# Hybrid attention block on one core: query and key projected with channels on partitions, rotated across partitions and carried to the scores through DRAM, the sliding heads placed amid the dilated pairs

## The chip, the core and the metric

The kernel runs on one core of one Trainium2 chip. The core has five engines with a program each: TensorE (PE, matmuls, with weight loads shown as PEld), VectorE (DVE), ScalarE (ACT), GpSimd (POOL) and SyncE (SP), which here issues every transfer between DRAM and on-chip memory. Sixteen DMA engines carry the transfers. Operands live in SBUF, matmul results in eight banks of PSUM. The metric is the device time of one execution in microseconds (us), the median of several runs.

## The reference

One layer of a decoder block: sequence 1024, width 1024, float32. Two sub-layers, each with an adaptive normalization ahead and a gated residual behind.

```python
h = rms_norm(x, g_attn_pre[l]) * (1 + sc_a) + sh_a
proj = h @ w_in[l]                       # 1024 x 2304
qa = partial_rope(proj[..., :o1] ...)    # mixer A: 8 query heads, 2 key heads, 2 value heads of 64
ka = partial_rope(...); va = ...
qb, kb = partial_rope(...), partial_rope(...); vb = ...   # mixer B: 8 heads of each
oa = banded_attention(qa, ka, va, 127, sink=sink_a[l])    # sliding window with sinks
ob = dilated_mixture_attention(qb, kb, vb)                # windows (128,1), (512,4), (2048,16)
mixed = concatenate([rms_norm(oa, g_mix_a[l]), rms_norm(ob, g_mix_b[l])])
y = mixed @ w_out[l]
x = x + gt_a * rms_norm(y, g_attn_post[l])
h = rms_norm(x, g_mlp_pre[l]) * (1 + sc_m) + sh_m
y = square(relu(h @ w_up[l])) @ w_down[l]
x = x + gt_m * rms_norm(y, g_mlp_post[l])
```

`partial_rope` turns the first 16 of the 64 channels of each head: channel f of the first eight is paired with channel f + 8, and both are mixed with the cosine and sine of the position. The dilated mixture is computed as one dense causal attention in which a mask adds the logarithm of the number of branches that see a key.

## The kernel before

Products are made in pairs of float32r halves: each operand is split into a high part and the rest, and three matmuls (high x high, high x low, low x high) stand for one. So a projection step over 128 of the 1024 channels (index k) is three matmuls.

The program isn't written in the order in which it runs. A planner (`Sched`, `run`) holds a queue of steps for each engine, with a duration, dependencies, buffers taken and given back (`Res`) and a priority, and writes the instructions out in the order of its own clock. PE has several streams (`dense`, `s`, `t`, `pv`, `post`, `misc` and others); `prefer` (L1932) chooses among them. SP's order is chosen in the same way, by the time at which a transfer can be issued. On the chip each engine then runs its list strictly in that order and waits where an operand isn't there. The planner counts a transfer as bytes over 345 GB/s plus fixed latencies.

The stages:

- To about 24 us: x is loaded, normalized and transposed to xnT; the modulation of the first sub-layer is computed on DVE (`mod_chunk`). The activations are kept in `hw` as [tile of 128 tokens][high, low].
- Input projection, 24 to 419 us. The output channels are cut into six units u of 384: units 0 to 3 hold two heads of mixer B each (two queries, two keys, two values), 4 and 5 one key head of mixer A with its four query heads. For each unit and each of eight tiles of 128 tokens, `proj_tile` (L805) makes [128 tokens x 384 channels] in one PSUM bank with 8 x 3 matmuls (`proj_mm`, L772): activations stationary, weights moving. `first_unit` (L783) does unit 0 over all eight banks as the activations become ready.
- `evac` (L673) empties each such bank: values are split into high and low parts (L687, L692); queries and keys are turned in place, channels along the free dimension (L703 to L707); they are split (L714 to L721); then PE transposes them to [channels x tokens], queries at L728 and keys at L740 (high and low parts, the key twice so that it fills 128 partitions), and ACT or DVE copies them to the rings `qring` and `kring`.
- Attention, mixed with the projection: 48 items. For mixer B an item is a pair of query blocks tp of one head h of unit u (`s_b`, L979), with pieces of up to 512 keys in two 256-wide halves (L1005); for mixer A it is one block of 128 queries for four heads (`s_a_`, L1038). Each goes through scores on PE, mask and maximum on DVE, exponential on ACT, normalization on POOL, then for each chunk of 256 keys (`t_pv`, L1097) four transposes (L1108 to L1115), a split (L1122, L1126) and the matmuls with the values (L1139 to L1150). Outputs go to DRAM (`o_dram`). The order of items (L955) is units 0 to 3, then the sliding heads, units 4 and 5.
- Output projection (`out_block`, L1294), eight blocks of tokens, each of 16 steps of three 512-wide matmuls (L1356 to L1358). Its weights are scaled and split into `hw` by `load_wo` (L1217), into the slot of each token tile once the last unit is done with that tile. A block starts when the items of its tokens are stored (`feed_out`, L1277).
- MLP, from 537.9 us: seven products for each of eight halves (`product`, L1746; L1780 to L1782), 512 wide. This change doesn't touch it.

POOL meanwhile computes the other modulation vectors from `w_ada` (`ada_piece`, L873).

## Time and profile before

| | us |
|---|---|
| runs | 1170.17, 1166.41, 1170.56 |
| median of 3 | 1170.17 |
| the profiled execution | 1170.0 |
| its span, first to last instruction | 1168.2 |
| PE busy in it | 1128.0 |
| DVE busy | 882.1 |
| ACT busy | 667.1 |
| POOL busy | 221.4 |
| bytes moved by DMA | 166.51 MB |

How to read the rows: a busy share says how long instructions were in flight, and matmuls overlap, so a PE that is busy isn't thereby at its peak; what a matmul costs in a stream is the distance from its start to the next start. "Idle before" in a group is the time for which the engine had nothing in flight just before these instructions, with what ended it. In the windows view each row is a stretch of the span with the busy time of each engine in it, the granted clock of PE (1.00 is full), the mean busy share of the 16 DMA engines, and the rate. In the DMA view a row gives the packets, their bytes, and for each kind of transfer the median time from its issue to its landing.

### The profile page before, as it was taken

How to read it: one execution, taken by the hardware profiler on the slowest of the kernel's cores; microseconds unless marked ns; L12 is line 12 of the kernel's file. 1: busy time of each engine (PE TensorE's matmuls, PEld its weight loads, DVE VectorE, ACT ScalarE, POOL GpSimd, SP SyncE). 2: the span in 40 equal slices, each digit the busy share in tenths (PEclk: the TensorE clock that was granted, in tenths of full speed). 3: DMA queues.
4: the chain of work that ended last, by engine and by line, in shares of the span. 5: the costliest groups of instructions: out<-in, count | busy, mean ns of one | idle time of the engine just before them, and what ended most of it. 6: DMA issues, size and time to landing. Idle time of an engine off the chain costs nothing.

```text
span 1168.2 us, 17209 instructions
## 1 busy us (share of the span) xinstructions
PE 1128.0 (97%) x5992; PEld 979.7 (84%) x5992; DVE 882.1 (76%) x1801; ACT 667.1 (57%) x1400; POOL 221.4 (19%) x270
## 2 busy tenths in 40 slices
PE   8989999999999979998999999999999999999996
PEld 6879999999999867887788888888888888888885
DVE  8987777777798996668969764499653796637998
ACT  7767666566667785666667434463234733256542
POOL 1044465555644431112000000000000000000002
PEclk9989999999999999999999999999999999999998
DMA  9613224222223324464584147922359311585103
GB/s 343 224 37 98 61 80 123 68 89 74 89 64 93 91 59 158 155 223 181 190 322 155 36 163 274 340 61 91 109 207 320 131 54 59 195 291 195 37 19 144
DMA packets 77542, 166.51 MB, mean 143 GB/s; under 512 B 6800, under 2 KB 27408, under 8 KB 77456
## 3 DMA queue, kind: packets, MB, share of 16 engines
q1 hardware_dynamic: 77456, 165.42, 41.4%
q8 instruction: 47, 0.77, 0.3%
q14 instruction: 39, 0.32, 0.1%
HBM read 137.08 MB, written 28.31 MB: 142 GB/s over the span
## 4 chain that ended last, share of the span: by engine, by line
PE 75%; DVE 13%; issue 4%; ACT 3%; POOL 2%; DMA 2%; SPq 0%; DVEq 0%; POOLq 0%; ACTq 0%
PE mlp_ps L1781 16%; PE mlp_ps L1782 16%; PE mlp_ps L1780 16%; PE pj L775 4%; PE pj L776 3%; PE pj L778 3%; PE s_ps L1005 3%; PE o_ps L1139 2%; PE pt_ps L1108 1%; PE pt_ps L1111 1%; DVE hw L1551 1%; PE pk L740 1%; DVE ph L1126 1%; PE y_ps L1356 1%; PE o_ps L1144 1%
## 5 line engine op out<-in xcount | busy, mean ns | idle before, releaser
L1780 PE MATMUL mlp_ps<-hw 128*128 128x512 f32 x896 | 350.3, 391 | 0.4 <-ACT hw L1542 0.4
L1781 PE MATMUL mlp_ps<-hw 128*128 128x512 f32 x896 | 349.1, 390 | 1.1 <-DVE hw L1548 1.1
L1782 PE MATMUL mlp_ps<-hw 128*128 128x512 f32 x896 | 348.9, 389 | 0.0
L1781 PEld LDWEIGHTS mlp_ps<-hw 128*128 128x128 f32 x896 | 168.5, 188 | 36.9 <-DVE hw L1548 1.4
L1780 PEld LDWEIGHTS mlp_ps<-hw 128*128 128x128 f32 x896 | 168.5, 188 | 36.1 <-ACT hw L1542 0.8
L1782 PEld LDWEIGHTS mlp_ps<-hw 128*128 128x128 f32 x896 | 168.4, 188 | 35.0
L1551 DVE TENSOR_TENSOR hw<-w,hw 128x1024 fp32r<-128x1024 f32 x96 | 114.6, 1220 | 94.7 <-ACT hw L1544 94.5
L1544 ACT CAST hw<-w 128x1024 fp32r<-128x1024 f32 x96 | 97.5, 1047 | 129.8 <-PE mlp_ps L1782 93.1
L1880 POOL TENSOR_TENSOR st<-st,nhalf 128x1 f32<-128x1 f32 x8 | 7.8, 979 | 602.8 <-DVE st L1878 602.8
L775 PE MATMUL pj<-w_hl,hw 128*128 128x384 f32 x320 | 118.2, 369 | 2.3 <-DVE sk L721 2.2
L776 PE MATMUL pj<-w_hl,hw 128*128 128x384 f32 x320 | 108.6, 339 | 1.2 <-DVE w_hl L497 1.1
L778 PE MATMUL pj<-w_hl,hw 128*128 128x384 f32 x320 | 108.5, 339 | 0.0
L1544 ACT CAST hw<-u 128x1024 fp32r<-128x1024 f32 x48 | 48.7, 1051 | 64.6 <-PE mlp_ps L1782 64.6
L1126 DVE TENSOR_TENSOR ph<-pt_ps,ph 128x512 fp32r<-128x512 f32 (+1 forms) x110 | 69.1, 643 | 17.6 <-ACT ph L1122 16.8
L1551 DVE TENSOR_TENSOR hw<-u,hw 128x1024 fp32r<-128x1024 f32 x48 | 57.0, 1218 | 18.2 <-ACT hw L1544 18.2
L1122 ACT CAST ph<-pt_ps 128x512 fp32r<-128x512 f32 (+1 forms) x110 | 59.3, 559 | 17.1 <-PE pt_ps L1111 13.3
L1035 POOL TENSOR_SCALAR p_sb<-p_sb,den 128x128 f32<-128x128 f32 (+3 forms) x64 | 51.3, 806 | 85.9 <-DVE den L1033 49.3
L1838 DVE TENSOR_TENSOR yacc<-yacc,mlp_ps 128x512 f32<-128x512 f32 x96 | 62.2, 681 | 3.3 <-PE mlp_ps L1782 3.3
L775 PEld LDWEIGHTS pj<-w_hl,hw 128*128 128x128 f32 x320 | 60.7, 190 | 3.6 <-DVE sk L721 3.1
L776 PEld LDWEIGHTS pj<-w_hl,hw 128*128 128x128 f32 x320 | 61.0, 191 | 2.7 <-DVE w_hl L497 2.1
L778 PEld LDWEIGHTS pj<-w_hl,hw 128*128 128x128 f32 x320 | 60.5, 189 | 0.0
L1030 ACT ACTIVATE p_sb<-p_sb,mn 128x128 f32<-128x128 f32 (+3 forms) x64 | 49.9, 780 | 17.4 <-DVE mn L1023 15.6
(206 smaller groups left out, 2167.3 us busy)
## 6 DMA issues: line engine op xcount, KB each, us to landing
hw<-s_dram SPq DMA_DIRECT2D x84, 512.0 KB, 4.4
wa_st<-in_w_ada SPq DMA_DIRECT2D x32, 512.0 KB, 4.3
w<-in_w_up SPq DMA_DIRECT2D x32, 512.0 KB, 5.2
w<-in_w_down SPq DMA_DIRECT2D x32, 512.0 KB, 7.7
s_dram<-hw SPq DMA_DIRECT2D x28, 512.0 KB, 3.8
w_st<-in_w_in SPq DMA_DIRECT2D x48, 192.0 KB, 3.8
x_sb<-in_x SPq DMA_DIRECT2D x16, 512.0 KB, 5.6
wa<-in_ada_t SPq DMA_DIRECT2D x16, 512.0 KB, 8.0
```

What stands on the lines that cost most here:

```text
L775: T.matmul(ps, hw[:, tb, 0, t], w[:, 0], start=(k == 0), stop=False)
L776: T.matmul(ps, hw[:, tb, 0, t], w[:, 1], start=False, stop=False)
L778: T.matmul(ps, hw[:, tb, 1, t], w[:, 0], start=False, stop=(k == KC - 1))
L1035: lambda b=b, qi=qi: G.tensor_scalar(rec.p[qi], rec.p[qi], b["den"][:], 1.0, ALU.mult, ALU.mult), [e], prio=1))
L1122: A.copy(b["ph"][:, 0, :w], b["pt"][:, :w])
L1126: V.tensor_tensor(b["ph"][:, 1, :w], b["pt"][:, :w], b["ph"][:, 0, :w].bitcast(F32), ALU.subtract)
L1544: A.copy(out[j][0], flat(src[j]))
L1551: V.tensor_tensor(out[j][1], flat(src[j]), out[j][0].bitcast(F32), ALU.subtract)
L1780: T.matmul(ps[m][:], sh, mh, start=starts and k == 0, stop=False, **kw)
L1781: T.matmul(ps[m][:], sh, ml_, start=False, stop=False, **kw)
L1782: T.matmul(ps[m][:], sl, mh, start=False, stop=k == 3, **kw)
L1838: e = op("DVE", t_dv(512), lambda: V.tensor_tensor(y(), y(), ps[m][:], ALU.add), [e, ml.e_y[tb, n]], gives=gives, prio=1)
```

## The change

Queries and keys are projected the other way round: weights stationary, activations moving, so that the result is [128 channels x 512 tokens] and no transpose by PE is needed. `hw` is now [channel chunk k][high, low][1024 tokens].

- The query and key channels of a unit form two chunks of 128 (`QUAD`: four heads, each chunk half of their channels); the two key heads of mixer A form one (`KEYS`). Units 0 to 3 have two query and two key heads in a QUAD, units 4 and 5 four query heads. A chunk is done in two halves of 512 tokens (`proj_chunk`, `chunk_mm`): 13 chunks, plus one for mixer A's values, which are transposed back by PE (`evac_va`, 16 transposes). Mixer B's values stay as before, [tokens x channels], but for two units at once, 256 wide (`proj_v`, `evac_v`). `first_unit` is now units 0 and 1's four chunks, in eight banks.
- The rows of a chunk are ordered so that the partner of each turned channel sits 64 partitions further. `evac_qk` turns them with 512-wide operations that read 64 (or 32) partitions and write the other half; the cosine and sine tables are laid out over partitions by way of DRAM (`cs_dram`).
- The turned halves are split and stored to `qk_dram`, high and low parts apart, in pieces of 16 rows of each head. `load_k` loads a key tile, 64 rows repeated onto 128 partitions, high and low each with one transfer; queries are loaded with high and low parts stacked. Rings: four key tiles of 512 tokens, four query tiles. A load waits for all stores of its unit and half. The factor -1/8 moves from the query copy into the mask step, whose masks are scaled by -8.
- Scores take up to 512 keys in one matmul. The items run in the order of units 0, 1, 4, 5, 2, 3; the projection in the order first unit, values, KEYS, values of A, 4, 5, 2, values, 3.
- Input weights come as 18 transfers of 512 KB instead of 48 of 192 KB, through the shared staging buffers, and their split's second half runs on DVE alone.
- `load_wo` replaces the activations chunk by chunk (`e_free`), which become free one after another in the last half-chunk of the projection. `prefer` now compares the share of projection left with the share of attention left, less a fifth.

The core of the diff:

```diff
+class Chunk:
+
+    def __init__(self, groups, turn=0):
+
+        self.rows, self.pieces, self.turn = [], [], turn
+        for heads, r0, n in groups:
+            p = len(self.rows)
+            self.rows += [(i, _DIMS[r0 + r]) for i in range(heads) for r in range(n)]
+            self.pieces.append((p, p + heads * n, heads, r0, n))
+
+_DIMS = [*range(0, 8), *range(48, 56), *range(16, 32), *range(8, 16), *range(56, 64), *range(32, 48)]
+QUAD = [Chunk([(4, 0, 16), (4, 32, 16)], 64), Chunk([(4, 16, 16), (4, 48, 16)])]
+KEYS = Chunk([(2, 0, 16), (2, 16, 16), (2, 32, 16), (2, 48, 16)], 32)
...
-    c[:, CW_MB:CW_MB + 1024] = neg[mult]
+    c[:, CW_MB:CW_MB + 1024] = -8.0 * neg[mult]
...
-    WR, WS, NP, NV, NK, NQ, NT, NO = 10, 5, 4, 21, 10, 12, 2, 6
+    WR, NP, NVA, NVB, NK, NQ, NT, NO, NSTG, NHL = 3, 4, 16, 8, 4, 4, 2, 6, 3, 2
...
+    cs_dram = [dram.tile([16, S], F32, name=f"cs_dram{i}") for i in range(3)]
+    qk_dram = [[dram.tile([2 if u == 6 else 4, 2, 64, 512], F32, name=f"qk_dram{u}_{i}") for i in range(2)]
+               for u in range(7)]
...
+    def split_ps(box, get_ps, deps, r_bank, prio, own=True):
+
+        def f_hi():
+            if own:
+                box["hl"] = prp.tile([P, 2, 512], F32R, name="hl", tag="hl", bufs=NHL)
+            A.copy(box["hl"][:, 0], get_ps())
+
+        def f_lo():
+            V.tensor_tensor(box["hl"][:, 1], get_ps(), box["hl"][:, 0].bitcast(F32), ALU.subtract)
+        e1 = op("ACT", t_ps(512), f_hi, deps + hl_turn * own, takes=[(r_split, 1)] * own, prio=prio)
+        if own:
+            hl_turn[:] = [e1]
+        return e1, op("DVE", t_dv(512), f_lo, [e1], gives=[(r_bank, 1)], prio=prio)
+
...
+    def evac_qk(u, ci, half, get_ps, done, r_bank, prio):
+        c = KEYS if u == 6 else QUAD[ci]
+        box = {}
+        e = done
+        if c.turn:
+            lo_, up = slice(0, c.turn), slice(64, 64 + c.turn)
+            rows = [slice(0, P)] if c.turn == 64 else [lo_, up]
+
+            def f_tt():
+                box["hl"] = prp.tile([P, 2, 512], F32R, name="hl", tag="hl", bufs=NHL)
+                t = box["t"] = box["hl"][:, 1].bitcast(F32)
+                ps, sn = get_ps(), cs_t[half][:, 1]
+                V.tensor_tensor(t[up], ps[lo_], sn[lo_], ALU.mult)
+                V.tensor_tensor(t[lo_], ps[up], sn[up], ALU.mult)
+
+            def f_rot():
+                ps, cn, t = get_ps(), cs_t[half][:, 0], box["t"]
+                for r in rows:
+                    V.tensor_tensor(ps[r], ps[r], cn[r], ALU.mult)
+                    V.tensor_tensor(ps[r], ps[r], t[r], ALU.add)
+            e = op("DVE", 2 * t_dv(512), f_tt, [done, e_cst[half]] + hl_turn, takes=[(r_split, 1)], prio=prio)
+            hl_turn[:] = [e]
+            e = op("DVE", 2 * len(rows) * t_dv(512), f_rot, [e], prio=prio)
+        es = split_ps(box, get_ps, [e], r_bank, prio, not c.turn)
+        e_w[u, ci, half] = []
+        for s in range(2):
+            def f_w(s=s):
+                for a, z, heads, r0, n in c.pieces:
+                    nc.sync.dma_start(qk_dram[u][half][0:heads, s, r0:r0 + n], box["hl"][a:z, s].bitcast(F32))
+            e_w[u, ci, half].append(load(f_w, 262144, [es[s]], gives=[(r_split, 1)] if s else [], prio=-300))
...
+    def load_k(key, u, half, row):
+
+        def emit():
+            t = k_t[key] = kring.tile([P, 2, 512], F32R, name="kt", tag="kt")
             for s in range(2):
+                nc.sync.dma_start(t[:, s].bitcast(F32),
+                                  qk_dram[u][half][row, s].unsqueeze(0).to_broadcast([2, 64, 512]))
+        k_e[key] = chained("k", emit, 524288, written(u, half), r_k)
...
+    def load_b(u, part=(0, 1)):
+        for i in part:
+            for j in range(2):
+                h, half = (i, j) if u < 3 else (j, i)
+                load_k((u, h, half), u, half, 2 + h)
+
+                def emit(h=j, half=i):
+                    t = q_t[u, h, half] = qring.tile([P, 512], F32R, name="qt", tag="qt")
+                    nc.sync.dma_start(t[:].bitcast(F32), qk_dram[u][half][h].rearrange("s r n -> (s r) n"))
+                q_e[u, j, i] = chained("q", emit, 262144, written(u, i), r_q)
+        st.posted.add(u)
...
+    def load_a(u):
+        for i in range(2):
+            load_k((u, i), 6, i, u - 4)
+        for qb in range(TB):
+            def emit(qb=qb):
+                t = q_t[u, qb] = qring.tile([P, 4, P], F32R, name="qt", tag="qt")
+                c = qb % 4 * P
+                nc.sync.dma_start(t[:].bitcast(F32),
+                                  qk_dram[u][qb // 4][:, :, :, c:c + P].rearrange("h s r n -> (s r) h n"))
+            q_e[u, qb] = chained("q", emit, 262144, written(u, qb // 4), r_q)
...
+    def evac_va(half, get_ps, done, r_bank, prio):
+        box = {}
+        es = split_ps(box, get_ps, [done], r_bank, prio)
...
+            def f_t(j=j):
+                box["ps", j] = px.tile([P, 4, P], F32R, name="pv", tag="x")
+                for i in range(2):
+                    for s in range(2):
+                        c = (2 * j + i) * P
+                        T.transpose(box["ps", j][:, 2 * i + s], box["hl"][:, s, c:c + P], ident_r[:])
+            e = pe_op("post", 0.24, f_t, [es[1], e_idr], takes=[(r_x, 1)], gives=[(r_split, 1)] if j else [])
...
+    def chunk_mm(ps, k, wt, c0, half, part):
+        t = slice(512 * half, 512 * half + 512)
         if part != 1:
+            T.matmul(ps, wt[:, 0, c0:c0 + P], hw[:, k, 0, t], start=(k == 0), stop=False)
+            T.matmul(ps, wt[:, 1, c0:c0 + P], hw[:, k, 0, t], start=False, stop=False)
         if part != 0:
+            T.matmul(ps, wt[:, 0, c0:c0 + P], hw[:, k, 1, t], start=False, stop=(k == KC - 1))
...
+        every = [(c, half) for c in (1, 0, 2, 3) for half in range(2)]
+        order = [(k, part, a) for k in range(AHEAD) for part in range(2) for a in every]
+        order += [(k, part, a) for a in every[:4] for k in range(AHEAD, KC) for part in range(2) if k + part < KC]
+        order += [(KC - 1, 1, a) for a in every[:4]]
+        order += [(k, part, a) for a in every[4:] for k in range(AHEAD, KC) for part in range(2)]
...
+    def proj_chunk(u, ci, wi, halves_=(0, 1), last=False):
+        for half in halves_:
+            b = []
+            for k in range(KC):
+                def emit(b=b, half=half, k=k):
+                    if k == 0:
+                        b.append(pj.tile([P, 512], F32, name="pj", tag="pj"))
+                    chunk_mm(b[0][:], k, w_hl[wi], k * P, half, None)
+
+                def after(k=k):
...
+                    if last:
+                        e_free[k].t, e_free[k].eng = sc.end, "PE"
+                d = dense(0.68, emit, w_e[wi], takes=[(r_pj, 1)] if k == 0 else [],
+                          gives=[(r_w, 1)] if half and k == KC - 1 else [], after=after)
...
+    todo_dense = [partial(proj_v, 0, tb, 4) for tb in range(TB)]
+    todo_dense += [partial(proj_chunk, 6, 0, 6), partial(proj_chunk, 6, None, 7)]
+    for u, w0 in ((4, 8), (5, 10), (2, 12)):
+        todo_dense += [partial(proj_chunk, u, c, w0 + c) for c in range(2)]
+        todo_dense += [partial(load_a if u >= 4 else load_b, u)]
+    todo_dense += [partial(proj_v, 1, tb, 14) for tb in range(TB)]
+    for half in range(2):
+        todo_dense += [partial(proj_chunk, 3, c, 16 + c, (half,), (c, half) == (1, 1)) for c in range(2)]
+        todo_dense += [partial(load_b, 3, (half,))]
...
+    items = []
+    for u in (0, 1, 4, 5, 2, 3):
+        if u >= 4:
+            items += [(u, qb) for qb in range(TB)]
+        elif u < 3:
+            items += [(u, tp, h) for tp, h in ((0, 0), (1, 0), (0, 1), (1, 1), (2, 0), (3, 0), (2, 1), (3, 1))]
+        else:
+            items += [(u, tp, h) for tp in range(4) for h in range(2)]
...
-                    for b0 in range(0, cw, 256):
-                        w = min(256, cw - b0)
-                        for hl in range(2):
-                            T.matmul(s[:, b0:b0 + w], toks[u, qb].q[h][:],
-                                     kts[u, (c0 + b0) // 256, h][:, hl, :w], start=(hl == 0), stop=(hl == 1))
-                d = 0.218 * -(-cw // 256)
-                deps = [toks[u, j].e_k for j in range(2 * tp, 2 * tp + 2)] + [toks[u, qb].e_q]
+                    for hl in range(2):
+                        T.matmul(s[:, :cw], q_t[u, h, qb // 4][:, qb % 4 * P:qb % 4 * P + P],
+                                 k_t[u, h, m][:, hl, :cw], start=(hl == 0), stop=(hl == 1))
+                d = 2 * max(0.0605, 0.00044 * cw)
+                deps = [q_e[u, h, qb // 4], k_e[u, h, m]]
...
-                    gives = [(r_q, 2)] + ([(r_k, 4)] if tp == 3 else [])
+                    gives = [(r_q, 1)] * (tp % 2) + [(r_k, 2)] * (tp == 3)
...
+    def can_start(it):
+        v = (it[0], 2 * it[1] + 1) if it[0] < 4 else (4, it[1])
+        return it[0] in st.posted and v in v_e
...
+                    A.mul(hw[:, k, 0], raw(), g)
...
-        if st.d < 5.9999 or not hasattr(ph2, "e_wo") or any(e.t is None for e in ph2.e_wo.values()):
...
-    LEAD = 0.5
+    KEEP = 0.20
 
     def prefer():
-        if st.d < 5.99 and st.d - st.a < LEAD:
+        if st.d < 5.99 and (DENSE - st.dense) / (DENSE - FIRST) > (1 - st.a / 6 - KEEP) / (1 - KEEP):
             return ("post", "misc", "mod", "fin", "xt", "dense", "pv", "s", "t")
         return ("post", "misc", "mod", "fin", "xt", "pv", "s", "t", "dense")
```

More of the change, by code (lines that the diff above doesn't have):

```diff
@@ L467, in hybrid_block @@
     x_t, x_e = {}, {}
-    IN_STG = (0, 1, 2)
+    IN_STG = (0, 1)
     def load_x(tb):
@@ new lines, in hybrid_block, with f_cd, f @@
+    e_sin = op("ACT", 3.4, f_sin, [e_ang, e_full[1]], prio=0)
+    fill = p0.tile([64, 2, P], F32, name="fill")
+    e_fill = op("DVE", 0.3, lambda: (V.memset(fill[:, 0], 1.0), V.memset(fill[:, 1], 0.0)), prio=6)
+    def f_cd(i):
+        def f():
+            d = cs_dram[i][:].rearrange("f (t n) -> t f n", n=P)
+            nc.sync.dma_start(d[:, 0:8], cs[:, i])
+            nc.sync.dma_start(d[:, 8:16], fill[:, min(i, 1)])
+        return f
+    e_cs = [load(f_cd(i), 65536, [e_sin, e_fill], prio=-500) for i in range(3)]
@@ L806, in proj_tile, with proj_v @@
+    e_free = [Ev() for _ in range(KC)]
+    def proj_v(u, tb, wi):
         b = []
```

482 lines of the change are left out of this document (230 added, 252 removed).

## The prediction

> **What bounds the kernel now.** I read the busy table first, then the windows by stage, the groups by line, the timeline for real spacings, the waits of PE, and last the DMA view. The page's busy line:
>
> ```profile
> PE 1128.0 (97%) x5992; PEld 979.7 (84%) x5992; DVE 882.1 (76%) x1801; ACT 667.1 (57%) x1400; POOL 221.4 (19%) x270
> ```
>
> TensorE (PE) is nearly never idle. The windows view, cut at the stages (columns: stretch, length, busy of PE, PEld, DVE, ACT, POOL, granted clock, DMA share, GB/s):
>
> ```profile
> 0.00:40.00 40.00, 33.40 (x187) 28.15 (x188) 35.55 (x90) 32.77 (x52) 5.11 (x12) 1.00 0.95 358
> 24.00:62.00 38.00, 35.20 (x198) 33.21 (x197) 36.53 (x73) 27.51 (x52) 0.00 (x0) 1.00 0.69 249
> 62.00:100.00 38.00, 32.46 (x227) 30.69 (x226) 30.05 (x120) 27.28 (x94) 14.40 (x18) 0.91 0.03 8
> 100.00:320.00 220.00, 218.39 (x1577) 211.51 (x1576) 162.08 (x556) 139.17 (x413) 124.80 (x135) 1.00 0.30 88
> 320.00:420.00 100.00, 95.22 (x628) 90.36 (x628) 90.97 (x310) 74.81 (x257) 41.30 (x59) 0.98 0.27 79
> 420.00:436.00 16.00, 11.00 (x68) 8.57 (x67) 14.46 (x41) 13.08 (x35) 7.16 (x10) 1.00 0.31 87
> ```
>
> From 24 to 436 us, input projection and attention run mixed, and PE is idle for 412 - 392.3 = 19.7 us: 5.5 in 62 to 100 (there at clock 0.91), 1.6 in 100 to 320, 4.8 in 320 to 420, 5.0 in the tail. Where these stages end and begin, from the views of single lines:
>
> ```profile
> L775 PE MATMUL acc<-w_hl,hw x64: 334/334/445, 23.6 to 61.5; 128*128 128x384 f32 x64
> L1780 PE MATMUL mlp_ps<-hw x896: 387/389/795, 537.9 to 1157.8; 128*128 128x512 f32 x180
> ```
>
> The change touches what lies ahead of 537.9 us, the start of the MLP. So I forecast that start, and carry its shift to the whole: span 1168.2, profiled execution 1170.0, which is also the median (1170.17).
>
> **PE, part by part.** Matmuls overlap, so their price is the distance of starts (timeline of PE):
>
> ```profile
> 201.26 0.51 PE L740 MATMUL pk<-ident_r,sk 128*128 128x128 f32 x4
> 201.61 0.41 PE L1108 MATMUL pt_ps<-head,p_sb 128*128 128x128 f32 x2
> ...
> 201.99 0.42 PE L775 MATMUL pj<-w_hl,hw 128*128 128x384 f32 x1
> 202.24 0.34 PE L776 MATMUL pj<-w_hl,hw 128*128 128x384 f32 x1
> ...
> 203.28 0.34 PE L778 MATMUL pj<-w_hl,hw 128*128 128x384 f32 x1
> ...
> 203.97 0.39 PE L1139 MATMUL o_ps<-ph,v_hl 128*128 128x256 f32 x2
> 204.20 0.40 PE L1144 MATMUL o_ps<-ph,v_hl 128*128 128x256 f32 x2
> ...
> 699.75 0.39 PE L1780 MATMUL mlp_ps<-hw 128*128 128x512 f32 x1
> ...
> 702.93 0.39 PE L1782 MATMUL mlp_ps<-hw 128*128 128x512 f32 x1
> ```
>
> A transpose costs 0.35/4 = 87 ns, a 384-wide matmul (203.28 to 203.97, four of them) 172 ns, a 256-wide one 0.23/2 = 115 ns, a 512-wide one 3.18/14 = 227 ns; the first one after another stream 250 instead of 172 ns.
>
> Transposes of q and k go (lines view):
>
> ```profile
> L740 PE MATMUL pk<-ident_r,sk 128*128 128x128 f32 x160 | 21.1, 247 | 2.5 <-ACT qt L733 2.1 <-DVE den L1089 0.4
> ...
> L728 PE MATMUL pq<-ident_r,sp 128*128 128x128 f32 x128 | 17.8, 242 | 3.1 <-DVE sp L720 2.2 <-ACT sk L715 0.7
> ```
>
> 288 x 87 ns = 25.1 us; 16 new ones for the sliding values give back 1.4: **-23.7**. Projection: 1152 matmuls x 172 = 198 us become 28 half-chunks x 24 x 227 plus 16 value tiles x 24 x 115 = 153 + 44 = 197: **0**. Score matmuls fall from 448 to 336 with the same columns: 0. 96 transpose groups less mean fewer returns to the projection, each 78 ns; half of them cost anything: **-4**. PE's waits for the copies around them:
>
> ```profile
> PE pq L728 <- DVE sp L720: 2.2, 3, 1.4
> PE pj L775 <- DVE sk L721: 2.2, 2, 1.7
> PE pk L740 <- ACT qt L733: 2.1, 1, 2.1
> ```
>
> **-6.5** for these three; and the 0.91 clock of 62 to 100 us (3.4 us) half regained, **-2**. The first stage becomes 192 x 227 = 43.5 us instead of 33, but that work is only moved ahead. Against it: the output weights can replace the activations only in the last half-chunk (per chunk k, not per finished token tile), and the last keys make a round trip; cover is two small items (some 7 us): **+5**. PE alone: -31.
>
> DVE: each half-chunk needs a 512-wide split, half of the QUAD ones four and each KEYS one six 512-wide operations more. The price row:
>
> ```profile
> L1126 DVE TENSOR_TENSOR ph<-pt_ps,ph 128x512 fp32r<-128x512 f32 x71 | 47.6, 681 | 7.7 <-ACT ph L1122 7.1
> ```
>
> (28 + 48 + 12) x 0.68 = 60, values 10: 70 us. From 62 to 436 DVE is busy for 297.6 of 374; with 70 more and nothing taken off, 368. So it would just fit, and the old rotation and splits of 48 tiles do go; ACT gets less. I take 0, and keep the upper end as a rival.
>
> **DMA, the new resource.** Queries and keys now go to DRAM and come back. Stores: 24 QUAD half-chunks x 2 (high, low) x 2 pieces of 4 heads x 16 rows, and 2 KEYS x 2 x 4 pieces of 2 heads x 16 rows; rows are 2 KB. Key loads: 20 tiles x 2 transfers of 256 KB, written as 2 copies x 64 rows. Query loads: 32 of 256 KB with 128 rows in front. What does the trace say on how a transfer is shared out? The DMA view of 88.5 to 92 us holds two stores of 64 rows and nothing else on the queue:
>
> ```profile
> DMA packets 161, 0.14 MB, mean 40 GB/s; under 512 B 32, under 2 KB 160, under 8 KB 160
> ...
> q1 hardware_dynamic: 160, 0.13, 15.7%
> ...
> o_dram<-ot SPq DMA_DIRECT2D x2, 64.0 KB, 2.0
> ```
>
> 128 row packets and 32 tiny ones: 16 shares for each transfer, ended by one packet each. Transfers of before have 64 or 128 rows as their outermost dimension, so 16 divides it. The new key loads begin with a dimension of 2 (a repeat), the stores with 4 or 2 heads. No row shows such a transfer. Two ends: it still runs in 16 shares; or the outermost dimension is what is cut, and a key load runs on 2 engines, a store on 4 or 2, the same ones each time. The nearest rows (these stores of 64 rows at 2.0 us, and, quoted below, a 256 KB load repeated over 128 partitions at 4.8 us) have a wide outermost dimension and can't tell. I take **the second end**: cutting the outermost dimension is the reading under which both sides of a transfer split into equal shares with one start address each.
>
> The Trainium skill states this very rule: "DMA: Bandwidth & Descriptors", sections "Why a DMA increments its semaphore by 16 and not by 1" and "Rules for kernel authors", says that the number of engines is the largest up to 16 that divides the slowest dimension of both sides, that the lowest-numbered engines are taken, and that a leading repeat of c copies confines a transfer to c engines. Two 16-share stores agree with it; no run here shows the small case.
>
> Price of the second end. Full rate is 358 GB/s at share 0.95 of 16 engines, 23.6 GB/s for one engine. On engines 0 and 1: 40 key loads x 131 KB = 5.56 us each, **222**; 96 QUAD store pieces x 32.8 KB = 1.39, **134**; 16 KEYS pieces x 1.39, **22**. The other traffic, spread over 16:
>
> ```profile
> DMA packets 19934, 28.90 MB, mean 77 GB/s; under 512 B 2019, under 2 KB 12323, under 8 KB 19892
> ...
> gate_st<-in_b_ada SPq DMA_DIRECT2D x2, 256.0 KB, 4.8
> ...
> gate_d<-gate_st SPq DMA_DIRECT2D x2, 256.0 KB, 2.5
> ```
>
> The first line is all of 62 to 436 us of before (its last two rows serve below); less 4.2 MB of output weights, plus 8.4 MB of queries: 33.1 MB / 16 / 23.6 = **88**. Together 466 us on one engine. The first accumulators are ready at about 23.6 + 43 - 5 + split 2 = 64 us; so the last key tile can't land before 64 + 466 = **530**. PE runs in order: behind that tile's scores stand the scores and values of the last two pairs of query blocks for both heads of the last unit (per head 3328 columns x 2 x 0.44 ns = 3, and 7 chunks x (four transposes 0.38 + four value matmuls 0.47) = 6, so 18 us for two), and the out projection, whose operands the order makes ready some 8 us after that tile: 384 x 227 = 87, its transposes and ends 12. MLP start 530 + 117 = 647 instead of 537.9: **+109**, 1279. SP is one queue too: a key load waits there for its stores to land, and output stores, weight and modulation loads stand behind it; key tiles are 4, one unit's, so a late unit delays the next loads. A few us of gaps are sure: **1282**.
>
> Its own range: 1235, if four of the eight out blocks (44 us) run ahead of the last tile; 1330, if a tenth of the 466 us passes with the engine idle.
>
> **Rivals.**
> - *All 16 engines share each transfer*: the other side. A key load lands in 2 to 5 us, one engine carries 28 + 33 + 3 + 88 = 152 us, and PE's sum holds: 1170 - 31 = **1139**, range 1122 to 1155. For it: DMA share 0.30 in 100 to 320 leaves room. The point: the last key tile would then be wanted at 507 - 117 = 390, 326 us after 64. Key loads cut by 8 would put 56 + 134 + 22 + 88 = 300 us on engine 0, which fits; cut by 4, 111 + 244 = 355, which doesn't. Above 4 shares the change is faster, below slower.
> - *16 engines, but landings later than the order assumes*: a 256 KB store took 2.5 and a 256 KB load 4.8 us; 1.5 us too late on each leg, on six units, gives back 18: **1157**.
> - *The bound only moves to DVE*: 368 of 374 us, nothing gained: **1170**.
>
> **How the numbers follow.** Confined transfers 0.58, all 16 engines 0.30, late landings 0.07, DVE 0.05. Forecast 1282. Faster by over 0.5% (about what a measurement can tell): 0.30 + 0.06 = 0.36; same 0.04; slower 0.60. The range for 8 in 10 must take in both signs: 1125 to 1330, which leaves out a tail of each (0.05 and 0.08).
>
> **What would show it.** Right: kt loads land 10 us or more after issue, fewer tiny packets than 16 for a transfer, PE idle in hundreds of short stretches released by DMA of kt, mean DMA share low all the same, PE's pq and pk gone, MLP start near 650. Wrong: kt lands in under 5 us, PE at 97%, MLP start near 507. It would be wrong too if the engines taken changed from transfer to transfer: then only latency is added, and the rival of late landings is near.

## The result, and the profile after

The kernel after takes 1376.41 us (median of 4 runs, 1375.11 to 1377.76) against 1169.47 us before (4 runs, 1166.41 to 1170.56): the ratio is 1.1775, with a 95% interval of 1.1747 to 1.1802, so **207 us slower**. The forecast was 1282, its range 1125 to 1330. Times here and below are medians of the executions in the chip's faster state; one execution of e14, 2019 us at a granted clock of 0.80, is left out for that reason.

The page of the kernel after; in order the busy line, the granted clock and the DMA share in 40 slices of 34 us, the packets, and the chain that ended last by engine:

```profile
PE 1138.8 (83%) x5512; PEld 953.8 (69%) x5512; DVE 855.0 (62%) x1499; ACT 616.7 (45%) x1089; POOL 208.5 (15%) x255
...
PEclk9986696796979879769999999999999999999999
DMA  9542432233444323321465482269224761259013
...
DMA packets 97097, 200.22 MB, mean 146 GB/s; under 512 B 7224, under 2 KB 30328, under 8 KB 97016
...
PE 56%; DMA 16%; SPq 9%; DVE 8%; POOL 3%; ACT 3%; issue 3%; DVEq 0%; POOLq 0%; ACTq 0%
```

PE has fallen from 97 to 83% of a longer span. From slice 3 to slice 18 (69 to 618 us) the granted clock is low again and again *and* the DMA share is low: PE starves, and the 16 engines are on average more than half empty meanwhile. The chain of waits now has 16% DMA and 9% SPq, which is time SP spends on issuing.

The windows by stage, cut as before, and the row of the MLP's first matmul line:

```profile
24.00:62.00 38.00, 36.70 (x162) 30.40 (x163) 32.68 (x45) 25.94 (x29) 0.00 (x0) 1.00 0.68 240
62.00:100.00 38.00, 24.61 (x154) 23.05 (x153) 15.41 (x27) 6.26 (x15) 15.35 (x15) 0.82 0.41 132
100.00:320.00 220.00, 121.72 (x628) 101.48 (x627) 83.21 (x212) 57.73 (x132) 59.60 (x66) 0.78 0.32 104
320.00:420.00 100.00, 67.52 (x371) 57.73 (x372) 58.19 (x174) 43.73 (x125) 32.51 (x45) 0.81 0.44 129
420.00:650.00 230.00, 161.78 (x944) 142.89 (x943) 125.24 (x359) 106.70 (x250) 71.05 (x87) 0.82 0.33 99
```

```profile
L1928 PE MATMUL mlp_ps<-hw x896: 387/389/795, 743.1 to 1363.0; 128*128 128x512 f32 x180
```

From 62 to 320 us PE is idle for 38 - 24.6 + 220 - 121.7 = 112 us, where it was 7 before, and DVE is no nearer to its limit than PE. The MLP starts at 743.1 us instead of 537.9 and lasts as long as before (620 us): the whole loss lies ahead of it.

What does the DMA queue do while all wait? The DMA view of 140 to 160 us, share and rate in 40 slices of half a microsecond, and SP's timeline at its start (start, length of issuing, line):

```profile
DMA  1111111118742222222222222222959832489879
GB/s 49 49 49 49 49 49 49 49 49 201 283 160 98 94 74 82 98 102 98 102 74 98 98 98 102 98 74 102 197 180 352 315 148 94 188 270 234 201 295 377
```

```profile
138.73 5.18 SPq L800 DMA_DIRECT2D qt<-qk_dram  x1
144.02 7.69 SPq L767 DMA_DIRECT2D qk_dram<-hl  x6
```

49 GB/s for 4.5 us is two engines at 24.5 each: the end of a key load. 98 GB/s is four engines: the stores of a half-chunk. Behind the key loads SP needs 5.18 us to issue one query load; 0.6 us is what a start takes where nothing is in the way (rows of e7, below). Who waits, from the waits of PE and, below it, of POOL and ACT (total, times, longest):

```profile
PE ada_ps L1041 <- POOL ada_acc L1025: 36.5, 4, 19.7
PE s_ps L1134 <- DMA qt<-qk_dram: 31.6, 4, 12.6
PE o_ps L1279 <- ACT ph L1252: 26.5, 2, 17.8
PE pj L939 <- DVE v_hl L829: 25.7, 3, 12.4
PE pt_ps L1238 <- POOL p_sb L1164: 24.6, 3, 21.9
PE o_ps L1268 <- ACT ph L1252: 21.6, 1, 21.6
PE s_ps L1134 <- DVE mn L1152: 21.0, 3, 14.0
PE s_ps L1134 <- DMA kt<-qk_dram: 13.8, 2, 8.9
```

```profile
POOL wa_st L1024 <- DMA wa_st<-in_w_ada: 174.6, 15, 30.2
```

```profile
ACT w_hl L528 <- DMA w_st<-in_w_in: 87.8, 9, 24.2
```

POOL's line in the kernel before:

```profile
POOL wa_st L894 <- DMA wa_st<-in_w_ada: 19.5, 8, 4.8
```

The key tile itself stands last among PE's waits of over 10 us, with 13.8. Most of the others go back to transfers that use all 16 engines: modulation loads awaited by POOL for up to 30 us, weight loads awaited by ACT for up to 24 us, query loads. POOL and ACT run in order, so `p_sb` and `ph`, which PE wants, stand behind such a wait. In the two longest waits of PE the load is late because SP starts it late. The first, 21.9 us for `p_sb`, ends at 236.0; POOL has waited until 231.1 for a modulation load that SP starts only at 219.2, behind a key tile and a query load:

```profile
203.20 10.65 SPq L788 DMA_DIRECT2D kt<-qk_dram  x2
213.91 5.18 SPq L800 DMA_DIRECT2D qt<-qk_dram  x1
219.19 0.49 SPq L1009 DMA_DIRECT2D wa_st<-in_w_ada  x1
```

The second, 21.6 us for `ph`, begins at 308.3; ACT has to get a weight load first that SP starts at 322.4.

### The profile page after: what moved, and what is told of

Same layout as the page of the kernel before. It is cut to its first block, busy times and chain, and to the rows that moved or that the text cites. A ratio compares the mean times of both kernels' runs of the same rounds, so it can differ in the third digit from the quotient of the medians.

```text
span 1373.5 us, 15914 instructions
## 1 busy us (share of the span) xinstructions
PE 1138.8 (83%) x5512; PEld 953.8 (69%) x5512; DVE 855.0 (62%) x1499; ACT 616.7 (45%) x1089; POOL 208.5 (15%) x255
## 2 busy tenths in 40 slices
DMA packets 97097, 200.22 MB, mean 146 GB/s; under 512 B 7224, under 2 KB 30328, under 8 KB 97016
## 4 chain that ended last, share of the span: by engine, by line
PE 56%; DMA 16%; SPq 9%; DVE 8%; POOL 3%; ACT 3%; issue 3%; DVEq 0%; POOLq 0%; ACTq 0%
PE mlp_ps L1930 14%; PE mlp_ps L1929 14%; PE mlp_ps L1928 14%; DMA wa_st<-in_w_ada 5%; SPq L788 4%; DMA qk_dram<-hl 3%; DMA w_st<-in_w_in 3%; SPq L800 2%; DMA qt<-qk_dram 2%; PE s_ps L1134 2%; DMA wo_st<-in_w_out 1%; PE pj L877 1%; PE pj L878 1%; PE pj L880 1%; POOL ada_acc L1025 1%
## 5 line engine op out<-in xcount | busy, mean ns | idle before, releaser
L1134 PE MATMUL s_ps<-kt,qt 128*128 128x512 f32 (+2 forms) x192 | 57.6, 408 | 66.3 <-DMA qt<-qk_dram 31.6
L1134 PEld LDWEIGHTS s_ps<-kt,qt 128*128 128x128 f32 x192 | 38.5, 225 | 73.8 <-issue 41.5
L877 PE MATMUL pj<-hw,w_hl 128*128 128x512 f32 x160 | 72.3, 452 | 0.0
L1152 DVE CUSTOM_DVE_ANT_0 p_sb<-s_ps,masks 128x512 f32<-128x512 f32 (+2 forms) x64 | 37.2, 586 | 48.2 <-PE s_ps L1134 46.1
L878 PE MATMUL pj<-hw,w_hl 128*128 128x512 f32 x160 | 66.4, 415 | 0.0
L880 PE MATMUL pj<-hw,w_hl 128*128 128x512 f32 x160 | 66.3, 414 | 0.0
L531 DVE TENSOR_TENSOR w_hl<-w_st,w_hl 128x1024 fp32r<-128x1024 f32 (+1 forms) x22 | 24.4, 1107 | 66.2 <-ACT w_hl L528 66.2
L1268 PE MATMUL o_ps<-ph,v_hl 128*128 128x256 f32 x160 | 40.0, 322 | 30.1 <-ACT ph L1252 21.6
```

The source lines that it names most:

```text
L877: T.matmul(ps, wt[:, 0, c0:c0 + P], hw[:, k, 0, t], start=(k == 0), stop=False)
L878: T.matmul(ps, wt[:, 1, c0:c0 + P], hw[:, k, 0, t], start=False, stop=False)
L880: T.matmul(ps, wt[:, 0, c0:c0 + P], hw[:, k, 1, t], start=False, stop=(k == KC - 1))
L1134: T.matmul(s[:, :cw], q_t[u, h, qb // 4][:, qb % 4 * P:qb % 4 * P + P], k_t[u, h, m][:, hl, :cw], start=(hl == 0), stop=(hl == 1))
```

## The experiments

Two causes had to be told apart from the start: the few engines that carry the round trip, and everything else of the change. Later the question was *how* the few engines cost so much more than their sum. All edits are to the kernel after, or to e7 where it is said.

**e1, e2, e3: widen both, only the key loads, only the stores.** Key loads, e1 and e2:

```diff
-                nc.sync.dma_start(t[:, s].bitcast(F32),
-                                  qk_dram[u][half][row, s].unsqueeze(0).to_broadcast([2, 64, 512]))
+                for c in range(2):
+                    nc.sync.dma_start(t[64 * c:64 * c + 64, s].bitcast(F32), qk_dram[u][half][row, s])
```

Stores, e1 and e3: the rows of a chunk are ordered by row and then by a pair of heads, the cosine and sine tables likewise, and a store takes two heads with its 16 rows outermost:

```diff
-                for a, z, heads, r0, n in c.pieces:
-                    nc.sync.dma_start(qk_dram[u][half][0:heads, s, r0:r0 + n], box["hl"][a:z, s].bitcast(F32))
+                for a, z, h0, r0, n in c.pieces:
+                    nc.sync.dma_start(qk_dram[u][half][h0:h0 + 2, s, r0:r0 + n].rearrange("h r n -> r h n"),
+                                      box["hl"][a:z, s].bitcast(F32))
```

> Key loads split into one transfer for each copy (64 rows outermost) and the stores into pieces of two heads with the 16 rows outermost; all else as after, same order on every engine. Theory (the few engines that carry the round trip are the whole loss): nothing is confined, an engine carries about 150 us instead of 466, the last key tile is no longer late, and the sum of the parts on PE holds: 1139 us, range 1122 to 1157, MLP start near 507, faster than before. Rival (the round trip itself is late, whatever engines carry it, because one queue issues and waits in order): key tiles still late, 1157 to 1250. Rival (DVE becomes the bound): 1170.

> Only the key loads widened (two transfers of 64 rows each to a half tile); stores still cut by 4 or 2. Theory: engine 0 carries 222/8 + 134 + 22 + 88 = 272 us in place of 466; with the same idle share as in after (the last tile landed 564 us after 64 where 466 were summed, a factor 1.21) 329 us, just what PE's order allows (326): 1139 to 1165. Rival (order of issue, not the load of engines): most of the 207 us stay, above 1280.

> Only the stores widened; key loads still on two engines. Theory: engine 0 carries 222 + (134 + 22)/8 + 88 = 330 us, by the factor 1.21 of after 400 us, last key tile at 464, MLP start 464 + 115 = 579, 1211 us (1165 to 1240). So the key loads alone cost 40 us over before, the stores alone next to nothing, and the two together 207. Rival (order of issue): above 1280.

Measured: e1 1195.05 us (1.0207 of before, 1.0186 to 1.0229), e2 1223.57 (1.0456, 1.0434 to 1.0477), e3 1355.59 (1.1581, 1.1562 to 1.1600). Widening all takes back 181 of 207 us, so the few engines are the cause; but e1 is still slower than before, where 1139 was expected. Widening the key loads alone takes back 153 us, the stores alone 21. That contradicts the sum in e3: the lowest engines carried 330 us in place of 466, and the time hardly moved.

**e4: half of the key loads.** The high half of the precision goes as in e2, the low half as in after.

> As after, but of each key tile only the low half of the precision still goes by the two-engine form (20 transfers); the high half goes as two transfers of 64 rows. Widening all 40 gave 153 us (1376 to 1224). Theory P (each two-engine load has its price, about 11 us a tile in series, paid one by one): half the gain, 1300 us (1285 to 1315). Theory R (the price comes from the queue being blocked once two such loads are outstanding on the same engines): one such load at a time is free to drain, so over three quarters of the gain, below 1262.

Measured: 1300.83 us (1.1121, 1.1093 to 1.1149). Half the loads, half the price (76 of 153 us), as theory P has it: each two-engine load is paid one by one, with no sign of a threshold.

**e5: weights, modulation and gate rows issued by ACT.**

```diff
-            nc.sync.dma_start(w_raw[i][:], w_in[i])
+            nc.scalar.dma_start(w_raw[i][:], w_in[i])
...
-            nc.sync.dma_start(ada.raw[i][:].rearrange("p (j n) -> p j n", j=2),
+            nc.scalar.dma_start(ada.raw[i][:].rearrange("p (j n) -> p j n", j=2),
```

> As after, every transfer in its form, but the weight, modulation and gate loads are issued by ACT's queue; SP keeps stores, key, query and output transfers. Theory H (head of line: SP stands blocked in key loads while loads that could run on idle engines queue behind it; POOL, ACT and then PE wait for those): the waits for ada_acc, p_sb and ph mostly go, below 1300 us. Theory K (the key tiles themselves land late and PE's order waits for them): 1350 to 1390.

Measured: 1339.64 us (1.1454, 1.1429 to 1.1479), 37 us less than after and between the two theories. ACT's wait for weight loads falls from the 87.8 us above to a fifth, but query loads and stores still wait on SP:

```profile
ACT w_hl L528 <- DMA qt<-qk_dram: 18.5, 1, 18.5
ACT w_hl L528 <- DMA w_st<-in_w_in: 18.2, 8, 4.1
```

The first row shows what blurs this experiment: ACT, which has to compute as well, now waits in its own list for transfers that SP has started (why, under e11).

**e6: the planner is told 11 us for a key tile.** The kernel's planner writes the order of all queues from durations, and has 524288 / 345000 = 1.5 us for a key tile.

```diff
-        k_e[key] = chained("k", emit, 524288, written(u, half), r_k)
+        k_e[key] = chained("k", emit, 11 * 345000, written(u, half), r_k)
```

> As after, every transfer in its form, but the planner is told 11 us for a key tile in place of 1.5 us, so that it writes another order on all queues. Theory O (the work would fit, only the order is written for loads of 1.5 us): below 1300. Theory K: the keys can't be had sooner whatever the order, 1330 to 1400.

Measured: 1302.83 us (1.1148, 1.1126 to 1.1171). The same transfers in another order cost 74 us less. So about a third of the loss is an order written for loads seven times faster than they are (the new order of e10 moved e7 by only 2 us). Line 788 of after and of e6 shows when the key loads were issued (min, median, max of one issue in ns, first and last start in us):

```profile
L788 SPq DMA_DIRECT2D kt<-qk_dram x40: 500/756/5826, 90.3 to 597.0; - x40
```

```profile
L788 SPq DMA_DIRECT2D kt<-qk_dram x40: 497/2334/7354, 91.0 to 527.9; - x40
```

The last one goes out 69 us earlier. Counted from the packets of the traces, no packet of the queue was in flight for 11% of 70 to 550 us in after, and for 1% in e6.

**e7: high and low part in one transfer, on e1.** 104 stores in place of 208 and 40 key loads in place of 80, all over 16 engines.

```diff
+                nc.sync.dma_start(t[64 * s:64 * s + 64].bitcast(F32), qk_dram[u][half][row].rearrange("s r n -> r s n"))
...
+                nc.sync.dma_start(qk_dram[u][half][h0:h0 + 2, :, r0:r0 + n].rearrange("h s r n -> r h s n"),
+                                  box["hl"][a:z].bitcast(F32))
```

> As e1_all16 (nothing confined), with high and low part in one transfer: 104 stores in place of 208, 40 key loads in place of 80. In e1 SP spends 139 us on issuing stores and 53 us on key loads. Theory S (what is left of the loss in e1 is SP's time to issue, which holds the two split buffers and so the accumulators): some 85 us of SP go, PE's idle time in 64 to 150 us (24 us, 6 in the kernel before) halves: about 1178 us. Rival D (the evacuation by DVE and the clock are the rest): within 0.5% of 1195.

Measured: 1158.30 us (0.9908, 0.9885 to 0.9930): 37 us less than e1, more than theory S asked for, and **0.9% faster than before**, which is little, but the interval excludes 1. The issues of e1, and those of e7 under them:

```profile
L768 SPq DMA_DIRECT2D qk_dram<-hl x208: 530/589/1746, 68.2 to 426.3; - x104
L791 SPq DMA_DIRECT2D kt<-qk_dram x80: 444/594/1192, 90.0 to 432.5; - x80
```

```profile
L767 SPq DMA_DIRECT2D qk_dram<-hl x104: 556/594/1592, 69.5 to 393.1; - x104
L789 SPq DMA_DIRECT2D kt<-qk_dram x40: 573/606/746, 86.0 to 398.2; - x40
```

A start of these stores and loads costs SP 0.6 us, for 64, 128 or 256 KB alike, and e1 has 144 more: 85 us of SP's time, of which 37 reach the end. SP issues 582 transfers in e7 and 580 in after, so after against e7 is nearly the pure price of the few engines: **218 us** (what else differs is that high and low part go together and how the rows of a chunk are ordered); and e7 against before is the rest of the change: **-11 us**.

**e8, e9: two pairs of the above.** e8 is e3 with e6's line, e9 is e5 with e6's line.

> The stores of e3_stores16 and the 11 us of e6_planned together: key loads on two engines, all else spread. Theory F (in e6 the lowest engines were never idle until the last key tile had landed at about 555 us, so their summed load is the floor there, and in after and e3 the order of 1.5 us kept them idle for the rest): the sum is 222 + 20 + 88 = 330 us, the floor 64 + 330 to 350 = 394 to 414, MLP start 510 to 530: 1145 to 1215 us, since the planner's one pipe is too slow for the other transfers. Rival (key tiles cost their 11 us in series with PE whatever else the engines carry): 1303 less the 21 us that e3 gained over after: about 1280.

> The loads on ACT's queue of e5_aside and the 11 us of e6_planned together; every transfer in after's form, so the two lowest engines carry the same bytes. Theory F (floor reached in e6): nothing more to gain, 1290 to 1310. Rival (the queue's blocking is a cost of its own, 37 us in e5): about 1266.

Measured: e8 1284.11 us (1.0962, 1.0932 to 1.0992), e9 1350.52 (1.1536, 1.1503 to 1.1568). e8 decides against theory F: 136 us less on the lowest engines bring 19 us, as the rival said. The sum of an engine's bytes was not what bound e6. In e9 both expectations fail, by 40 us and more. Two waits of ACT point to why it loses 48 us to e6: ACT issues the loads there, and an exponential (`p_sb`) and splits (`ph`) stand behind its waits for SP's transfers:

```profile
ACT p_sb L1159 <- DMA qk_dram<-hl: 29.5, 1, 29.5
ACT ph L1252 <- DMA kt<-qk_dram: 26.4, 2, 17.4
```

No run tests whether that is the whole of the 48 us.

**e10: e7 with a planner that knows 0.6 us for each start.**

> e7_merged with the planner told that SP needs 0.6 us for each start (4 in a store of a half chunk, 2 in a key tile) in place of 0.48 us for the whole group. If the stalls that remain in e7 come from an order written for a faster SP: 1145 to 1156. If not: within 0.5% of 1158.

Measured: 1156.25 us (0.9870, 0.9840 to 0.9900). That is within 0.5% of e7 and no proof of more, but it is the fastest of all, 14 us under before.

**e11: the few engines loaded with transfers that nothing reads, on e7.**

```diff
+            for s in range(2):
+                z = dram.tile([2, 64, 512], F32, name=f"z{len(k_t)}_{s}")
+                nc.sync.dma_start(z[:], qk_dram[u][half][row, s].unsqueeze(0).to_broadcast([2, 64, 512]))
```

> e7_merged (nothing confined, 1158 us) with two transfers added behind the loads of each key tile: the two-engine form of after's key loads, 2 copies of 64 rows, 256 KB each, into DRAM that nothing reads; 40 in all, some 24 us of SP's time to issue. The lowest engines get back the 222 us of after's key loads, but no key tile waits for them. Theory B (what counts is that every other transfer also has a share on the two lowest engines and lands only behind what stands there): over 100 us of the 153 come back, above 1260. Theory S (what counts is that the key tile itself is 11 us late, tile after tile): less than 40 us, below 1200.

Measured: 1329.41 us (1.1357, 1.1338 to 1.1376), **171 us more than e7**, as theory B forecast: the key tiles go over 16 engines as in e7, nothing reads the added bytes, and the loss is there again. The row of the added line, then two waits that grew, of e11 and of e7:

```profile
L792 SPq DMA_DIRECT2D z<-qk_dram x40: 578/593/642, 87.5 to 552.0; - x40
```

```profile
POOL wa_st L1027 <- DMA wa_st<-in_w_ada: 112.2, 13, 23.9
```

```profile
ACT w_hl L529 <- DMA w_st<-in_w_in: 72.1, 9, 21.6
```

```profile
POOL wa_st L1024 <- DMA wa_st<-in_w_ada: 38.9, 11, 7.4
```

```profile
ACT w_hl L529 <- DMA w_st<-in_w_in: 25.1, 10, 8.6
```

(Each share of an added transfer is two packets of 64 KB, 2.42 us each by the packets of the trace, so 4.84 us a transfer and 9.7 us a pair.)

The path to the loss has two links, and the semaphore events of the trace show both. First, a transfer over 16 engines lands late through its shares on the two lowest ones. From its start to its last share a query load takes 12.5 us in the median, where e7 has 4.1, a key load 8.3 in place of 5.1; of the 104 stores 37 have their last two shares more than 1 us behind the other fourteen, by up to 19.8 us. So the key tile is late here too, and e11 doesn't separate theory B from theory S as cleanly as it was meant to.

Second, SP waits for landings. In all runs the starts take eight semaphores in turn (in e5 and e9 SP and ACT share them), and nearly every start carries a wait until the transfer of eight starts before, on the same semaphore, has landed. So SP does wait for the added transfers: 33 times between 60 us and the first matmul of the MLP, 126 us in all. Three rows of SP's waits:

```profile
SPq L767 <- DMA z<-qk_dram: 42.8, 12, 4.6
SPq L1332 <- DMA z<-qk_dram: 18.6, 5, 4.7
SPq L1312 <- DMA z<-qk_dram: 14.7, 3, 5.8
```

No issue of the added line takes over 642 ns, but single stores take up to 6.3 us to issue and single query loads up to 8.0. What stands behind in SP's list starts late: of the 13 weight loads after 60 us the third goes out at 147.9 us, in e7 at 112.0, while only three of the 13 have their last two shares more than 1 us late. So e11 doesn't clear SP's blocking: SP is held here as well.

**e12: five key tiles in place of four.** The room for it comes from the output tiles, and from four small scratch buffers in place of six.

```diff
-    WR, NP, NVA, NVB, NK, NQ, NT, NO, NSTG, NHL = 3, 4, 16, 8, 4, 4, 2, 6, 3, 2
+    WR, NP, NVA, NVB, NK, NQ, NT, NO, NSTG, NHL = 3, 4, 16, 8, 5, 4, 2, 3, 3, 2
```

> after with five key tiles in place of four (room for it: three output tiles in place of six, four small scratch buffers in place of six); every transfer in after's form. Theory G (a late tile costs its 11 us because its buffer comes free only when the unit before is done): one tile of each unit comes earlier, 25 to 45 us less, 1330 to 1350. Theory B (a queue of two engines behind which everything stands): within 15 us of 1376, or slower.

Measured: 1374.82 us (1.1748, 1.1731 to 1.1766), no change. It is what theory B forecast but doesn't settle it, since the shorter ring of output tiles brought a wait of its own on DVE:

```profile
DVE ot L1322 <- DMA o_dram<-ot: 62.4, 7, 27.5
```

**e13, e14: the same load in short pieces, on e7.** 166 small transfers (160 were reckoned), one behind each group of stores, query load, weight or modulation load and output store; two engines in e13, and in e14, where the 16 rows stand outermost, all. The line of e13:

```diff
+        nc.sync.dma_start(z[:], x[0:16, 0:512].unsqueeze(0).to_broadcast([2, 16, 512]))
```

> e7_merged with 160 small transfers that nothing reads (two copies of 16 rows of 2 KB, into DRAM), one behind each group of stores, each query load, each weight or modulation load and each output store: two-engine form, 16 packets of 84 ns = 1.34 us on each of the two, 215 us in all, where e11 had 9.7 us at a time and 194 in all for 171 us of loss. Theory Q (what costs is the length of the queue in front of a transfer that is awaited; 1.3 us is hidden by PE's slack): at most 40 us above e14. Theory T (the sum counts): 130 us or more above e14.

> The same 160 transfers at the same places with the 16 rows outermost, so that each engine gets two packets. It prices the 96 us of SP's time that the 160 starts take: e1 against e7 (some 150 starts more, 37 us) says 1158 + 20 to 40 = 1178 to 1198.

Measured: e13 1240.95 us (1.0595, 1.0567 to 1.0623), e14 1187.71 (1.0144, 1.0118 to 1.0169). The 166 starts cost 29 us, 0.18 each. Confining them costs 53 us more, outside the bounds of both theories (40 and 130) and much nearer to theory Q.

With e14's price of a start, the prices of confined time come together. e2 has 40 more starts than after, so widening the key loads is worth 153 + 7 = 160 us; e3 has 106 more (96 stores, 10 for tables), so the stores are worth 21 + 19 = 40 us; e11 has 40 more than e7, which leaves 171 - 7 = 164 us (estimates from e14's 0.18 us). The last column is counted from the traces: by how much longer SP was held, that is, between 60 us and the first matmul of the MLP, its waits for landings and what each of its issues took beyond 0.7 us.

| what is confined | time on the lowest engines, us | at a time, us | loss, us | loss per us | SP held longer by, us |
|---|---|---|---|---|---|
| e11 against e7, unread, behind each key tile | 194 | 9.7 | 164 | 0.85 | 164 |
| key loads, after against e2 | 222 | 11.1 | 160 | 0.72 | 166 |
| stores, after against e3 | 156 | 1.4 a piece | 40 | 0.26 | 43 |
| e13 against e14, unread, scattered | 223 | 1.3 | 53 | 0.24 | 52 |

A microsecond on the lowest engines costs a quarter where it comes in pieces of 1.3 us, and some three quarters or more where 10 us stand together. A microsecond for which SP is held costs a whole one in all four rows. The same holds for the whole: SP is held for 241 us in after and for 24 in e7, 217 more for 218 us of loss. Its waits for the other engines hardly shrink meanwhile (281 us in e7, 261 in e11, 285 in after), so nothing takes the time up. This is a count and not an experiment: no run changes SP's semaphores alone. And it holds only while the planner's order stays: in e6, which has another, SP is held for 266 us and only 145 are lost to e7.

## Why the prediction was right and wrong

- **The share of engines: right.** The chosen end, that the outermost dimension is what is cut, is exact. The packets under 512 B end one share each: 96 QUAD stores x 4 + 16 KEYS stores x 2 + 40 key loads x 2 + 13 loads and stores of tables and positions, 88, and 415 others x 16 make 7224, the number of the page. The Trainium skill has this rule ("DMA: Bandwidth & Descriptors", section "Why a DMA increments its semaphore by 16 and not by 1"); the trace agrees to the packet. The rate of one engine, put at 23.6 GB/s, is 24.5.
- **The side, and where the loss lies: right.** Slower, all of it ahead of the MLP. The tail of 117 us holds nearly: the DMA view of 596 to 640 us (40 slices of 1.1 us) has the last stretch of two engines, 46 to 54 GB/s, end at 619, and the MLP starts 124 us later.

```profile
GB/s 60 246 45 50 50 48 48 48 48 50 50 209 328 275 135 54 48 50 48 54 46 3 42 227 236 32 0 0 0 15 56 4 0 0 0 60 0 0 0 0
```

- **The size: wrong, in one term.** The failing step reads "so the last key tile can't land before 64 + 466 = 530", closed by "A few us of gaps are sure". The sum of bytes on engine 0 is a floor, and it was priced as if it were the time, with 3 us for everything that SP's one queue adds. The tile landed at 617 (the last event of its semaphore): 87 us later; for 54 us of 64 to 619 no packet of the queue was in flight at all. What the runs showed in its place is the term of 3 us: SP was held for 241 us in after and for 24 in e7, where nothing is confined, and 218 us lie between the two. The prediction had named this path ("output stores, weight and modulation loads stand behind it") and put nearly nothing on it. e3 and e8 show that the sum didn't bind (466 down to 330, and 21 and 19 us gained); e6 shows that 74 us were the order, written for 1.5 us a tile; e11 shows that confined bytes cost 171 us even where no key load is confined. The upper end of 1330 allowed a tenth of 466 us idle, where nearly a fifth was needed.
- **The signs to look for: half wrong.** "PE idle in hundreds of short stretches released by DMA of kt" did not come. PE's waits for `kt` are two, 13.8 us; the loss is in some twenty waits of up to 22 us, mostly for POOL, ACT and DVE. The MLP starts at 743, not near 650. "kt loads land 10 us or more after issue" did come: the DMA view gives no landing times for after, but by the semaphore events a key load lands 8.1 to 21.0 us after its start, 15.4 in the median.
- **PE's sum: mis-sized.** e7 is the change without confinement. Its MLP starts here:

```profile
L1928 PE MATMUL mlp_ps<-hw x896: 387/389/795, 529.4 to 1149.3; 128*128 128x512 f32 x180
```

  8.5 us earlier than before, not 31. The rows of e7 for 62 to 420 us (before's stand in the prediction) say where most of the 22 went:

```profile
62.00:100.00 38.00, 31.69 (x211) 29.50 (x210) 21.05 (x42) 9.03 (x25) 16.60 (x16) 0.91 0.83 232
100.00:320.00 220.00, 206.43 (x1210) 174.13 (x1211) 175.35 (x488) 129.08 (x335) 117.99 (x147) 0.98 0.66 187
320.00:420.00 100.00, 92.27 (x577) 80.92 (x576) 78.44 (x213) 64.72 (x141) 41.78 (x47) 0.97 0.48 134
```

  PE is idle for 27.6 us there, 11.9 before: 16 us of new waits. The granted clock is 0.98 and 0.97 where it was 1.00 and 0.98, which is 220 x 0.02 + 100 x 0.01 = 5 us. The matmuls are gone as counted (5512 in place of 5992: 272 transposes, 112 score matmuls and 96 of the projection fewer); in place of the waits that went, PE waits for DVE (`ph` 7.2 us, `v_hl` 5.4, `mn` 2.6), POOL (`p_sb` 2.5) and one query load (2.1).
- **DVE at 0: right.** It is busy for 275 of 358 us in e7, less than the 283 of before, far from the 368 of 374 feared for 62 to 436 us. That rival is out.
- **The rival of 16 engines, 1139: right in sign only with few starts.** e7 is at 1158 and e1, with 144 starts more, on the slow side of before at 1195. The prediction let SP's issues cost nothing. The break-even "above 4 shares" was drawn from the sum, so it falls with it; no kernel with 4 or 8 shares was run. The Trainium skill ("DMA: Bandwidth & Descriptors", section "Rules for kernel authors") advises one large transfer in place of many small ones; e1 against e7 agrees, at 37 us.

Open: how much of e9's 48 us ACT's waits are, what eight semaphores in turn cost by themselves, how much of the price in after the ring of four key tiles has, and what the new place of the sliding heads in the order is worth, which no run changed by itself.

## What to carry to other kernels

Before a tensor is sent through DRAM, look at the outermost dimension of both sides of each transfer: where it is 2 or 4, put rows there, and merge transfers so that the count doesn't rise. A transfer on few engines isn't priced by its own bytes: ask what else has a share on those engines, how many microseconds stand in front of it at a time, and for which landings the issuing engine itself waits, since everything behind in its list then starts late. And where a planner writes the order, a wrong duration in it costs too (74 of 218 us here).

## What the runs showed of the hardware

- 194 us of transfers that nothing reads, on two of 16 engines, cost 171 us on a kernel whose other transfers used all engines (e11).
- SP's issue of a transfer takes 0.3 to 0.6 us in the median of each line of e7 ahead of the MLP. In after, where much stands on the two lowest engines, a key load takes up to 5.8 us to issue and a query load up to 7.4. In e11 the confined transfers themselves (two packets of 64 KB to a share) are issued within 0.64 us, but single stores take up to 6.3 and query loads up to 8.0.
- A transfer over 16 engines can land with its last two shares far behind the others: up to 19.8 us for a store of e11, 1.4 in e7.
- A packet of 2 KB takes 84 ns, one of 64 KB 2.42 us: 24.4 and 27 GB/s on one engine.
- Where PE waits, its granted clock falls too: 0.78 in 100 to 320 us of after, 0.98 there in e7. For the same 5512 matmuls it is busy for 1138.8 us in after and 1109.9 in e7, so part of what a stall costs seems to come that way.
